# A two-layer decoder step on one core: the dilated attention's last part, the samples' attention and the first output weights in one weave

## The chip, the core and the metric

The kernel runs on one core of a Trainium2 chip. The metric is the device time of one execution in microseconds; the kernel before took 1539.32 us in the median of three runs (1535.01 to 1544.55). The engines are named as in the profile: PE (TensorE, matmuls; PEld its weight loads), DVE (VectorE), ACT (ScalarE), POOL (GpSimd), SP (SyncE, which here only issues DMAs). Each takes its instructions in the order in which they stand in its queue.

## What is computed

Two layers run over 1024 prompt tokens and 32 sample tokens (8 sequences of 4). The first layer is attention. Its path A looks 128 tokens back; its path B has three groups with dilations 1, 4 and 16, whose outputs are merged by their softmax denominators. Cut to what matters here:

```python
def _layer0_out(x, oa, obs, lses, z, w_out, ln_g, ln_b):
    wts = softmax(stack(lses, 0), 0)                    # the three groups of B
    ob = einsum('rbshg,rbshgd->bshgd', wts, stack(obs, 0))
    mix = concatenate([oa.reshape(..), ob.reshape(..)], -1)
    mix = mix * silu(z)                                 # gate path
    y = einsum('bse,ed->bsd', mix, w_out)               # output projection
    return layer_norm(DN_ALPHA * x + y, ln_g, ln_b)
```

The prompt's tokens attend to each other. The samples' tokens attend to caches (128 keys for A and for B's first group, 128 of each dilated one) and to themselves, with the same weights and the same output projection. The second layer (mLSTM) follows.

## The kernel before, in words

All matmuls on activations split each operand into a rounded high part and a rest, and add three products: high by high, high by low, low by high. The tokens lie in three chunks (`CH`): 384, 384 and 288, the last with the 32 samples.

Layer 0 first projects keys and values, then queries (`proj_q`). Path A and the row maxima of B's groups 1 and 2 are woven with the query projections. A second weave (`W2`) joins the gate path (`proj_z0`, 8 feature blocks) with `attention_b`: the maxima of group 3, B's scores for kv=0, and `EARLY` = 9 query blocks of kv=1 (`self.late`). A third weave (`W3`) joins the rest of kv=1, the samples' attention (`sample_attn`) and six merges. Then `out0` loads and splits the eight output weights (`load_wo`) and runs the output projection (`out_proj`, L862) over nine token tiles.

`weave` only fixes the order in which the program's parts are recorded, by shares of work; `ahead` gives a part a priority. A scheduler then makes the order on each engine from priorities, dependencies and its own durations, so the engine order is not that of the code.

For B, `scores` (L462) takes one query block at a time. It loads a mask row for it (`mask_load`, L442: 2 KB into the last partition of `EM`, two buffers in turn, twice 1x4x128). For each of one or two key blocks it runs three matmuls into `sc` (L475, mask L457 or L460, L477), two exponentials on ACT (`ph`, `p`, L481 and L482), the low part `pl` on DVE or, every fourth time, on POOL (L116, L484), and three matmuls into `av` (L488 to L490). `emit` then adds `av` into the result `OD` on DVE (L580, L582). There are 35 such score blocks for each kv, 70 in all. `AB_PS` says which PSUM tags hold `sc` and `av`: four and two buffers in the second weave, two and three in the third. A load of queries (`Q`, 512 KB) serves two query blocks.

The result goes to DRAM chunk by chunk and comes back in `merge0` (L816): `mo` (result), `mf` (denominators, whose reciprocal is taken on DVE, L839, for kv=1), `mz` (gate), a product, then its high part on ACT (`mh`) and its low part on DVE (`ml`). Merges are named by (path, kv, chunk); those of path 1 (B), kv=1, come from `last` when a chunk is finished.

The samples' attention loads the cached keys and values for four sequences at a time into `KT` tiles (`sample_keys`, L660, pool `smt`, 4 buffers). Scores go into `sS` (L682) and through DVE masks; transposes (`pT`, L709 and L710) and values (`so`, L724 and L729) follow, and a transpose back (`oT`, L742).

All DMAs of this part are issued from SP, in the order of its queue; a DMA whose wait is not over holds back those behind it.

Of the kernel before, what the change touches and what calls it, by code (L numbers as in the profile page):

```python
# [4 lines left out]
F32 = mybir.dt.float32  # L5
# [59 lines left out]
W1, W2, W3, W4 = (129, 76), (86, 80), (28, 15, 6), (64, 90)  # L65

EARLY = 9
# [5 lines left out]
ENG = dict(q="scalar", z="scalar")  # L73
# [24 lines left out]
class Builder:  # L98
# [409 lines left out]
    def finish(self, ty, kv, sink_nm=None):  # L508

        nc = self.nc  # L510
        dn = self.sm.tile([32, 128], F32, tag="dn", name="dn")
# [56 lines left out]
    def attn_b(self, kv, done=None):  # L568
# [3 lines left out]
        for g in (3, 2, 1):  # L572
            (K1, K2), V = self.k_load(g, kv), self.v_load(g, kv)

            def emit(qb, av, g=g):
# [7 lines left out]
                if g == 1 and qb in (2, 5, 7):  # L583
                    t = slice(CH[qb // 3][0], 128 * qb + 128)
                    self.store('o', self.OD[1][kv][:, :, t], OD[:, :, t])
                    if done:
                        done(qb // 3)
# [72 lines left out]
    def sample_keys(self, src, g, a, st):  # L660

        out = []
        if g < 2:
            t = st.tile([128, 4, 128], F32, tag="KT", name="KT")
            self.load(t, src[:, 4 * a:4 * a + 4])
            return [t[:, j:j + 1] for j in range(4)]
        for u in range(2):
            t = st.tile([128, 2, 4, 128], F32, tag="KT", name="KT")
# [5 lines left out]
    def sample_group(self, g, st):  # L674

        nc, A = self.nc, self.A
        for a in range(2):
            ks = self.sample_keys(A['kt'][g], g, a, st)
# [24 lines left out]
    def sample_av(self, g, o, sp, st, first, last):  # L703
# [18 lines left out]
        for a in range(2):  # L722
            vs = self.sample_keys(A['vc'][g], g, a, st)
# [26 lines left out]
    def sample_attn(self, sp, st):  # L750
        nc = self.nc
        self.sample_queries(sp)
# [3 lines left out]
        for ty, gs in ((0, (0,)), (1, (1, 2, 3))):  # L756
            for g in gs:
                yield from self.sample_group(g, st)
# [21 lines left out]
            for i, g in enumerate(gs):  # L780
                yield from self.sample_av(g, o, sp, st, i == 0, g == gs[-1])
# [104 lines left out]
    def layer0(self):  # L886
# [24 lines left out]
        with tc.tile_pool(name="qp", bufs=2) as self.qp, tc.tile_pool(name="kp", bufs=2) as self.kp, \  # L911
                tc.tile_pool(name="vp", bufs=2) as self.vp, tc.tile_pool(name="ppool", bufs=3) as self.ppool, \
                tc.tile_pool(name="odp", bufs=1) as self.odp:
            sm = self.sm = tc.alloc_tile_pool(name="sm", bufs=1)
# [11 lines left out]
            self.KZ = [sm.tile([128, TP], F32R, name=f"KZ{u}") for u in range(2)]  # L926
# [4 lines left out]
            self.maskm = sm.tile([128, 4, 128], F32R, name="maskm")  # L931
            self.hi(self.maskm, raw[:, 0:512].rearrange("p (u k) -> p u k", u=4))
            self.EM = [sm.tile([128, 2, 4, 128], F32R, name=f"EM{u}") for u in range(2)]
# [34 lines left out]
            def attention_b():  # L968
# [3 lines left out]
                self.bps = AB_PS[1]  # L972
                yield from self.attn_b(0)
                late = self.late = self.attn_b(1, last)
                for _ in range(EARLY):
                    yield next(late)

            weave((gate_path(), W2[0]), (ahead(tc, attention_b(), AHEAD[1]), W2[1]))
# [3 lines left out]
            self.x2p = tc.alloc_tile_pool(name="x2p", bufs=1, side="right")  # L982
            self.mp = tc.alloc_tile_pool(name="mp", bufs=1, side="right")
            sm.release()
            M = self.M = [(self.xp.tile([128, 8, n], F32R, tag=f"xh{c}", name=f"mh{c}"),
                           self.xp.tile([128, 8, n], F32R, tag=f"xl{c}", name=f"ml{c}"))
                          for c, (t0, n) in enumerate(CH)]

            def merges(cs):
                for c in cs:  # L990
                    for ty, kv in ((0, 0), (0, 1), (1, 0)):
                        self.merge0(ty, kv, c, M)
                        yield 1.0

            self.bps = AB_PS[2]
            with tc.tile_pool(name="smt", bufs=4) as st:
                sp = Scratch(*(self.x2p.tile([128, 3072], F32, tag=f"x{u}x2", name=f"scr{u}") for u in "hl"))
                weave((ahead(tc, self.late, AHEAD[2]), W3[0]), (ahead(tc, self.sample_attn(sp, st), AHEAD[2]), W3[1]),
                      (merges((0, 1)), W3[2]))
            self.merge0(1, 1, 2, M, False)  # L1000
            run(merges((2,)))

    def out0(self):
# [3 lines left out]
        self.wsp = tc.alloc_tile_pool(name="wsp1", bufs=2, side="right")  # L1007
        with tc.tile_pool(name="wo", bufs=1) as wp:
            W = [self.load_wo(A['wo0'], k, *self.wo_tiles(wp, k)) for k in range(8)]
# [629 lines left out]
```

## Time and profile before

| what | before |
|---|---|
| time, median of 3 runs (range) | 1539.32 us (1535.01 to 1544.55) |
| profiled execution, its own time | 1543.16 us |
| its span | 1541.4 us |
| mean granted TensorE clock | 0.961 |
| PE busy | 1431.8 us (93%) |
| DVE busy | 894.1 us (58%) |
| ACT busy | 482.0 us (31%) |
| DMA | 227.33 MB, 147 GB/s in the mean |

The profile shows one execution. Busy times of PE are modelled and overlap in a pipeline, so a matmul's duration is longer than the step to the next one. A granted clock of 1.0 is the upper level (2.4 GHz), 0.5 the lower (1.2 GHz).

### The profile page before, as it was taken

The page shows a single profiled execution, that of the slowest core. Times are in us where ns is not written, and L with a number is a line of the kernel's source. Part 1 is how long each engine was busy: PE and PEld are TensorE (multiplying, and loading weights), DVE is VectorE, ACT ScalarE, POOL GpSimd, SP SyncE. Part 2 cuts the span into 40 slices and gives each one's busy share as a digit, 9 for nine tenths or more (in the row PEclk, how much of TensorE's full clock was granted, in tenths as well). Part 3 has the DMA queues.
Part 4 walks back from the last instruction along what each step waited for, and adds up shares of the span by engine and source line. Part 5 has one row for each costly group of instructions (what it writes and reads, how often), then busy time and mean ns, then how long its engine had stood idle before and what let it go on. Part 6 is the DMA issues. An engine that isn't in the chain of part 4 may idle for free.

```text
span 1541.4 us, 22195 instructions
## 1 busy us (share of the span) xinstructions
PE 1431.8 (93%) x7908; PEld 1216.0 (79%) x7908; DVE 894.1 (58%) x2483; ACT 482.0 (31%) x907; POOL 173.9 (11%) x213
## 2 busy tenths in 40 slices
PE   8998999999897889568999999999999999999997
PEld 8988998889897555136879878888898899877785
DVE  4312455558676777635776436555565565556686
ACT  5332134342122656212104313332233133323310
POOL 1003131212220222000000000000000000000010
PEclk9999999999999989658999999999999999999999
DMA  8444555547753565765311375374214322341741
GB/s 293 166 152 157 191 179 163 166 140 219 198 169 94 174 193 162 220 203 192 124 52 57 118 254 190 117 232 140 77 46 150 109 60 63 109 135 22 233 129 53
DMA packets 140220, 227.33 MB, mean 147 GB/s; under 512 B 17616, under 2 KB 108080, under 8 KB 139592
## 3 DMA queue, kind: packets, MB, share of 16 engines
q1 hardware_dynamic: 132046, 204.55, 43.0%
q10 hardware_dynamic: 8064, 21.37, 3.8%
q8 instruction: 63, 1.03, 0.3%
q14 instruction: 47, 0.39, 0.1%
HBM read 167.06 MB, written 81.88 MB: 162 GB/s over the span
## 4 chain that ended last, share of the span: by engine, by line
PE 70%; DMA 15%; DVE 7%; issue 4%; ACT 2%; POOL 1%; SPq 1%; DVEq 0%; ACTq 0%; POOLq 0%
PE pj L199 10%; PE pj L200 10%; PE pj L201 10%; PE py L165 4%; PE py L166 4%; PE py L167 3%; PE pvo L165 3%; PE pvo L166 3%; PE pvo L167 3%; DMA G<-GR 2%; DMA QZ<-QQ 2%; DMA wr<-in_wo_dram 1%; PE av L488 1%; PE sc L475 1%; PE av L489 1%
## 5 line engine op out<-in xcount | busy, mean ns | idle before, releaser
L199 PE MATMUL pj<-xh,wh 128*128 128x384 f32 (+1 forms) x576 | 188.9, 328 | 9.8 <-DVE sl L117 5.5
L199 PE MATMUL pj<-x1h,wh 128*128 128x384 f32 (+1 forms) x576 | 189.9, 330 | 1.7 <-ACT QT L1166 1.6
L201 PE MATMUL pj<-x1h,wl 128*128 128x384 f32 (+1 forms) x576 | 188.1, 327 | 0.0
L200 PE MATMUL pj<-xl,wh 128*128 128x384 f32 (+1 forms) x576 | 187.9, 326 | 0.0
L200 PE MATMUL pj<-x1l,wh 128*128 128x384 f32 (+1 forms) x576 | 187.7, 326 | 0.0
L201 PE MATMUL pj<-xh,wl 128*128 128x384 f32 (+1 forms) x576 | 187.6, 326 | 0.0
L199 PEld LDWEIGHTS pj<-xh,wh 128*128 128x128 f32 x576 | 110.2, 191 | 14.7 <-DVE sl L117 6.4
L199 PEld LDWEIGHTS pj<-x1h,wh 128*128 128x128 f32 x576 | 108.9, 189 | 6.5 <-issue 3.3
L201 PEld LDWEIGHTS pj<-x1h,wl 128*128 128x128 f32 x576 | 108.7, 189 | 6.0 <-issue 5.8
L200 PEld LDWEIGHTS pj<-x1l,wh 128*128 128x128 f32 x576 | 108.9, 189 | 4.0 <-issue 3.8
L201 PEld LDWEIGHTS pj<-xh,wl 128*128 128x128 f32 x576 | 110.0, 191 | 1.0
L200 PEld LDWEIGHTS pj<-xl,wh 128*128 128x128 f32 x576 | 110.0, 191 | 0.8
L429 DVE CUSTOM_DVE_ANT_0 junk<-st,maskq 128x256 f32<-128x256 f32 (+1 forms) x256 | 93.2, 364 | 24.6 <-PE st L425 9.7
L165 PE MATMUL pvo<-voh,x1h 128*128 128x512 f32 x256 | 101.1, 398 | 2.3 <-DVE SZ L1182 2.3
L166 PE MATMUL pvo<-voh,x1l 128*128 128x512 f32 x256 | 100.4, 395 | 0.0
L167 PE MATMUL pvo<-vol,x1h 128*128 128x512 f32 x256 | 99.6, 392 | 0.0
L481 ACT ACTIVATE ph<-sc 128x512 fp32r<-128x512 f32 x100 | 60.1, 602 | 76.8 <-PE sc L477 60.5
L808 POOL TENSOR_TENSOR rsw<-rsw,mhalf 128x1 f32<-128x1 f32 (+1 forms) x54 | 40.5, 750 | 354.7 <-DVE rsw L807 340.5
L122 POOL TENSOR_TENSOR wl<-wr,wh 128x1024 fp32r<-128x1024 f32 x24 | 58.6, 2443 | 183.2 <-ACT qs L233 136.4
L112 ACT ACTIVATE wh<-wr 128x1024 fp32r<-128x1024 f32 x48 | 50.8, 1058 | 78.3 <-PE pj L200 71.1
L116 DVE TENSOR_TENSOR pl<-p,ph 128x512 fp32r<-128x512 f32 x82 | 59.9, 737 | 20.0 <-ACT p L482 18.1
L425 PE MATMUL st<-K,QZ 128*128 128x256 f32 x256 | 51.7, 289 | 9.7 <-DMA QZ<-QQ 4.9
(352 smaller groups left out, 3129.8 us busy)
## 6 DMA issues: line engine op xcount, KB each, us to landing
Q<-QQ SPq DMA_DIRECT2D x32, 512.0 KB
out_kvs_dram<-in_cache_b_kv_dram SPq DMA_DIRECT2D x16, 1022.0 KB
wr<-in_w0f_dram SPq DMA_DIRECT2D x24, 512.0 KB
wr<-in_w1f_dram SPq DMA_DIRECT2D x24, 512.0 KB
QQ<-sh ACTq DMA_DIRECT2D x16, 512.0 KB
QQ<-sl ACTq DMA_DIRECT2D x16, 512.0 KB
QZ<-QQ SPq DMA_DIRECT2D x32, 256.0 KB
wr<-in_wo_dram SPq DMA_DIRECT2D x16, 512.0 KB
```

What stands on the lines that cost most here:

```text
L112: return self.nc.scalar.activation(out, in_, AF.Copy, scale=scale)
L116: return self.nc.vector.tensor_tensor(out, in_, f(hi), OP.subtract)
L122: self.nc.gpsimd.tensor_tensor(out, in_, f(hi), OP.subtract)
L165: nc.tensor.matmul(ps, xh[:, k, t], wh, start=k == 0, stop=False)
L166: nc.tensor.matmul(ps, xl[:, k, t], wh, start=False, stop=False)
L167: nc.tensor.matmul(ps, xh[:, k, t], wl, start=False, stop=k == 7)
L199: nc.tensor.matmul(ps[:, :n], wh[:, k, :], xh[:, k, :n], start=k == 0, stop=False)
L200: nc.tensor.matmul(ps[:, :n], wh[:, k, :], xl[:, k, :n], start=False, stop=False)
L201: nc.tensor.matmul(ps[:, :n], wl[:, k, :], xh[:, k, :n], start=False, stop=k == 7)
L425: nc.tensor.matmul(st[:, u, :], Q1[:, h, q0:q0 + 128], K1[:, w0:w0 + 256], start=True, stop=True)
L429: nc.vector.tensor_tensor_reduce(junk[:, :n], st[:, u, c0:c0 + n], mk, 1.0, -3e38, OP.add, OP.max, ST[:, 8 * h + qb:8 * h + qb + 1])
L481: nc.scalar.activation(ph, sc, AF.Exp)
```

## The change

`KZ`, `EM` and `maskm` (the key tiles for low parts, the mask rows with their one-hot matrices, and the mask matrices) move from the pool `sm` into a pool `mk` that is released only after B. So `sm` can go before B, which makes room for the merge pool, and for `wsp1`, the pool of weight tiles, which was allocated in `out0`. The second weave now holds only the gate path and the maxima of group 3. The third weave holds all of B (both kv), the samples' attention, the first two output weights and the six merges of chunks 0 and 1. All of B runs with two `sc` buffers and three `av` buffers. The samples' `KT` tiles take the weight tiles of `wsp1` (tags `wh` and `wl` in turn, two buffers each). The first two output weights sit in the same pool. The denominators for kv=0 use a `wraw` tile. The stores of B's result move from SP's queue to ACT's.

```diff
-W1, W2, W3, W4 = (129, 76), (86, 80), (28, 15, 6), (64, 90)
-EARLY = 9
+W1, W2, W3, W4 = (129, 76), (86, 8), (77, 20, 8), (64, 90)
...
-ENG = dict(q="scalar", z="scalar")
+ENG = dict(q="scalar", z="scalar", b="scalar")
...
-        dn = self.sm.tile([32, 128], F32, tag="dn", name="dn")
+        dn = (self.wraw if ty else self.sm).tile([32, 128], F32, tag="wraw" if ty else "dn", name="dn")
...
-                    self.store('o', self.OD[1][kv][:, :, t], OD[:, :, t])
+                    self.store('b', self.OD[1][kv][:, :, t], OD[:, :, t])
...
-    def sample_keys(self, src, g, a, st):
+    def sample_keys(self, src, g, a):
+        def tile(shape):
+            self.nkt += 1
+            return self.wsp.tile(shape, F32, tag="wh" if self.nkt % 2 else "wl", name="KT")
...
+            mk = tc.alloc_tile_pool(name="mk", bufs=1)
...
-            self.KZ = [sm.tile([128, TP], F32R, name=f"KZ{u}") for u in range(2)]
+            self.KZ = [mk.tile([128, TP], F32R, name=f"KZ{u}") for u in range(2)]
...
-            self.maskm = sm.tile([128, 4, 128], F32R, name="maskm")
+            self.maskm = mk.tile([128, 4, 128], F32R, name="maskm")
...
-            self.EM = [sm.tile([128, 2, 4, 128], F32R, name=f"EM{u}") for u in range(2)]
+            self.EM = [mk.tile([128, 2, 4, 128], F32R, name=f"EM{u}") for u in range(2)]
...
-            def attention_b():
+            def maxima_b():
                 for kv in range(2):
                     yield from self.attn_b_stats(3, kv)
                     self.attn_b_max(kv)
-                self.bps = AB_PS[1]
-                yield from self.attn_b(0)
-                late = self.late = self.attn_b(1, last)
-                for _ in range(EARLY):
-                    yield next(late)
-
-            weave((gate_path(), W2[0]), (ahead(tc, attention_b(), AHEAD[1]), W2[1]))
+
+            weave((gate_path(), W2[0]), (ahead(tc, maxima_b(), AHEAD[1]), W2[1]))
             tmp.release()
             stage.release()
             self.wsp.release()
             self.x2p = tc.alloc_tile_pool(name="x2p", bufs=1, side="right")
+            self.wsp = tc.alloc_tile_pool(name="wsp1", bufs=2, side="right")
+            sm.release()
             self.mp = tc.alloc_tile_pool(name="mp", bufs=1, side="right")
-            sm.release()
...
+            self.halves = 0
+
+            def attention_b():
+                for kv in range(2):
+                    yield from self.attn_b(kv, last if kv else None)
+                    self.halves += 1
 
             def merges(cs):
-                for c in cs:
-                    for ty, kv in ((0, 0), (0, 1), (1, 0)):
+                for ty, kv in ((0, 0), (0, 1), (1, 0)):
+                    while self.halves < ty:
+                        yield None
+                    for c in cs:
                         self.merge0(ty, kv, c, M)
                         yield 1.0
 
+            def samples():
+                sp = Scratch(*(self.x2p.tile([128, 3072], F32, tag=f"x{u}x2", name=f"scr{u}") for u in "hl"))
+                yield from self.sample_attn(sp)
+                for k in range(2):
+                    w = [self.wsp.tile([128, 1024], F32R, tag=f"w{u}", name=f"o{u}") for u in "hl"]
+                    self.W0.append(self.load_wo(A['wo0'], k, *w))
+                    yield 0.5
+
+            self.W0 = []
             self.bps = AB_PS[2]
-            with tc.tile_pool(name="smt", bufs=4) as st:
-                sp = Scratch(*(self.x2p.tile([128, 3072], F32, tag=f"x{u}x2", name=f"scr{u}") for u in "hl"))
-                weave((ahead(tc, self.late, AHEAD[2]), W3[0]), (ahead(tc, self.sample_attn(sp, st), AHEAD[2]), W3[1]),
-                      (merges((0, 1)), W3[2]))
+            weave((ahead(tc, attention_b(), AHEAD[1]), W3[0]), (ahead(tc, samples(), AHEAD[2]), W3[1]),
+                  (ahead(tc, merges((0, 1)), AHEAD[1]), W3[2]))
             self.merge0(1, 1, 2, M, False)
             run(merges((2,)))
+            mk.release()
...
-            W = [self.load_wo(A['wo0'], k, *self.wo_tiles(wp, k)) for k in range(8)]
+            W = self.W0 + [self.load_wo(A['wo0'], k, *self.wo_tiles(wp, k)) for k in range(2, 8)]
```

What the scheduler makes of it is seen at three places. Line numbers of the changed kernel differ by a few. On PE, at the end of B, the order before is this (the `sS`, `pT` and `so` rows are the samples'):

```order
L477 MATMUL sc<-Q_6351,KZ_955 128x512
L488 MATMUL av<-ph,V 66x512
L489 MATMUL av<-ph,V 64x512
L682 MATMUL sS<-KT,scrh 32x128 x8
L490 MATMUL av<-pl,V 66x512 x2
L488 MATMUL av<-ph,V 66x512
L489 MATMUL av<-ph,V 64x512
L490 MATMUL av<-pl,V 66x512
L709 MATMUL pT<-ident,scrl 128x128
L710 MATMUL pT<-ident,scrl 32x128
```

All but the first eight matmuls of the samples on cached keys stand behind B's last value matmul. On PE, at the start of kv=1 (group 3), the order of the changed kernel is this:

```order
L475 MATMUL sc<-Q_5609,KZ_957 128x512
L684 MATMUL sS<-KT,scrl 32x512 x2
L488 MATMUL av<-pl,V 66x512
L486 MATMUL av<-ph,V 66x512
L487 MATMUL av<-ph,V 64x512
L684 MATMUL sS<-KT,scrl 32x512 x2
L473 MATMUL sc<-Q_5700,K_5690 128x512
L684 MATMUL sS<-KT,scrl 32x512 x2
L455 MATMUL sc<-EM_965,maskm 128x4x64 x2
L475 MATMUL sc<-Q_5700,KZ_958 128x512
```

The samples' scores stand in ones and twos between B's, and so do their transposes and values further on. On SP, at the same place, the order of the changed kernel is this (`KT` 128x1024 is 512 KB, `Q` the queries, `EM` a mask row):

```order
L104 DMA Q_5700<-QQ_78 128x4x256
L104 DMA KT<-in_kt_dram 128x1024 x2
L104 DMA EM_965<-QQ_78 1x4x128
L104 DMA KT<-in_kt_dram 128x1024
L104 DMA EM_965<-QQ_78 1x4x128
L104 DMA KT<-in_kt_dram 128x1024
L104 DMA EM_966<-QQ_78 1x4x128 x2
L104 DMA Q_5766<-QQ_78 128x4x256
L104 DMA KT<-in_kt_dram 128x1024 x3
L104 DMA EM_965<-QQ_78 1x4x128 x2
```

Before, these loads stood behind B's last mask row on SP; now seven of the eight large key loads are in this piece. On PE, at the end of B, the order of the changed kernel is this (`py` is the output projection; eleven more rows of it stand ahead of the first):

```order
L165 MATMUL py<-ol,mh_4914 128x512
L488 MATMUL av<-pl,V 66x512
L163 MATMUL py<-oh,mh_4914 128x512
L164 MATMUL py<-oh,ml_4915 128x512
L165 MATMUL py<-ol,mh_4914 128x512
L163 MATMUL py<-oh,mh_4914 128x512
L164 MATMUL py<-oh,ml_4915 128x512
L165 MATMUL py<-ol,mh_4914 128x512
L488 MATMUL av<-pl,V 66x512
L486 MATMUL av<-ph,V 66x512
L487 MATMUL av<-ph,V 64x512
L488 MATMUL av<-pl,V 66x512
```

The projection with weights 0 and 1 (24 matmuls over tiles 0 and 1 and two column halves) begins ahead of B's last five value matmuls; before, it began behind the samples' last transpose `oT`.

## Rows read from the trace of the kernel before

**Rows 1.** The page: the span, and two rows of the 40 slices.
```profile
span 1541.4 us, 22195 instructions
...
PE   8998999999897889568999999999999999999997
...
PEclk9999999999999989658999999999999999999999
```

**Rows 2.** Busy time by stage: window, length, engines, granted clock, DMA share, GB/s.
```profile
core 0: us, PE busy (x) PEld busy (x) DVE busy (x) ACT busy (x) POOL busy (x), PEclk, DMA share, GB/s
...
500.00:565.00 65.00, 55.44 (x212) 34.76 (x212) 47.19 (x69) 40.72 (x75) 16.17 (x14) 0.92 0.66 190
565.00:621.00 56.00, 49.98 (x202) 32.51 (x201) 37.73 (x58) 35.26 (x65) 11.34 (x9) 0.92 0.57 160
621.00:632.00 11.00, 3.52 (x21) 1.29 (x21) 10.02 (x12) 0.55 (x2) 1.26 (x1) 0.69 0.60 183
632.00:694.00 62.00, 35.32 (x245) 15.48 (x246) 29.79 (x62) 11.92 (x34) 3.06 (x2) 0.56 0.70 219
694.00:725.00 31.00, 25.71 (x97) 20.17 (x97) 13.27 (x18) 8.67 (x10) 0.52 (x1) 0.84 0.60 200
```

**Rows 3.** The same view in windows of 10 us.
```profile
580.00:590.00 10.00, 8.73 (x42) 5.78 (x42) 5.21 (x11) 6.33 (x12) 2.37 (x2) 1.00 0.99 263
...
650.00:660.00 10.00, 5.55 (x14) 0.82 (x16) 3.30 (x9) 0.04 (x1) 1.80 (x1) 0.62 0.94 294
```

**Rows 4.** The chain that ended last: start, length, what.
```profile
499.04 1.75 DMA EM<-QQ
...
547.73 4.98 DMA EM<-QQ
...
632.98 4.27 DMA mf<-OD
...
647.07 8.47 DMA KT<-in_kt_dram
...
677.38 5.54 DMA KT<-in_vc_dram
...
695.63 9.32 DMA wr<-in_wo_dram
```

**Rows 5.** ACT in order of time: start, length, engine, line.
```profile
499.62 0.33 ACTq L109 DMA_DIRECT2D SZ<-sz  x1
...
620.79 0.59 ACT L482 ACTIVATE p<-sc 128x512 f32<-128x512 f32 x1
```

**Rows 6.** PE in order of time.
```profile
605.49 0.39 PE L475 MATMUL sc<-Q,K 128*128 128x512 f32 x1
...
619.41 0.40 PE L475 MATMUL sc<-Q,K 128*128 128x512 f32 x1
...
723.70 1.07 PE L167 MATMUL py<-ol,mh 128*128 128x512 f32 x4
```

**Rows 7.** DVE in order of time.
```profile
632.71 0.96 DVE L117 SCALAR_TENSOR_TENSOR ml<-mz,mh 128x768 fp32r<-128x768 f32 x1
...
637.27 4.96 DVE L839 RECIPROCAL mf<-mf 128x384 f32<-128x384 f32 x2 [3.46 <-DMA mf<-OD]
...
663.20 1.75 DVE L839 RECIPROCAL mf<-mf 128x256 f32<-128x256 f32 x1 [0.36 <-DMA mf<-OD]
...
694.38 1.22 DVE L116 TENSOR_TENSOR ol<-wr,oh 128x1024 fp32r<-128x1024 f32 x1
```

**Rows 8.** SP's issues in order of time.
```profile
546.34 0.43 SPq L106 DMA_DIRECT2D mz<-SZ  x1
547.08 0.56 SPq L106 DMA_DIRECT2D mo<-OD  x1
```

**Rows 9.** DMA issues from 480 to 720 us: count, KB each.
```profile
KT<-in_kt_dram SPq DMA_DIRECT2D x8, 512.0 KB
...
KT<-in_kt_dram SPq DMA_DIRECT2D x4, 256.0 KB
```

More of the change, by code (lines that the diff above doesn't have):

```diff
@@ L658, in sample_queries @@
             self.smx.append(sp.tile([128, 2], F32, tag=f"sm{g}", name="smx"))
-    def sample_keys(self, src, g, a, st):
+    def sample_keys(self, src, g, a):
+        def tile(shape):
+            self.nkt += 1
+            return self.wsp.tile(shape, F32, tag="wh" if self.nkt % 2 else "wl", name="KT")
         out = []
         if g < 2:
-            t = st.tile([128, 4, 128], F32, tag="KT", name="KT")
+            t = tile([128, 4, 128])
             self.load(t, src[:, 4 * a:4 * a + 4])
@@ L667, in sample_keys @@
         for u in range(2):
-            t = st.tile([128, 2, 4, 128], F32, tag="KT", name="KT")
+            t = tile([128, 2, 4, 128])
             s = 4 * a + 2 * u
@@ L672, in sample_keys, with sample_group @@
         return out
-    def sample_group(self, g, st):
+    def sample_group(self, g):
         nc, A = self.nc, self.A
         for a in range(2):
-            ks = self.sample_keys(A['kt'][g], g, a, st)
+            ks = self.sample_keys(A['kt'][g], g, a)
             w = 128 * (1 if g < 2 else 4)
@@ L701, in sample_exp, with sample_av @@
                                  accum_out=den[:, a:a + 1])
-    def sample_av(self, g, o, sp, st, first, last):
+    def sample_av(self, g, o, sp, first, last):
         nc, A = self.nc, self.A
@@ L722, in sample_av @@
         for a in range(2):
-            vs = self.sample_keys(A['vc'][g], g, a, st)
+            vs = self.sample_keys(A['vc'][g], g, a)
             nc.tensor.matmul(o[:, a, :], pN[:, 128 * a:128 * a + 128], self.VS[:, 128 * g:128 * g + 128],
@@ L748, in sample_out, with sample_attn @@
                 nc.vector.tensor_copy(dst.rearrange("p c (s t) -> p c s t", t=4), src)
-    def sample_attn(self, sp, st):
+    def sample_attn(self, sp):
         nc = self.nc
+        self.nkt = 0
         self.sample_queries(sp)
@@ L757, in sample_attn @@
             for g in gs:
-                yield from self.sample_group(g, st)
+                yield from self.sample_group(g)
             m = self.smx[gs[0]]
@@ L780, in sample_attn @@
             for i, g in enumerate(gs):
-                yield from self.sample_av(g, o, sp, st, i == 0, g == gs[-1])
+                yield from self.sample_av(g, o, sp, i == 0, g == gs[-1])
             self.sample_out(o, rec, ty, sp)
@@ L1006, in out0 @@
         self.mp.release()
-        self.wsp = tc.alloc_tile_pool(name="wsp1", bufs=2, side="right")
         with tc.tile_pool(name="wo", bufs=1) as wp:
-            W = [self.load_wo(A['wo0'], k, *self.wo_tiles(wp, k)) for k in range(8)]
+            W = self.W0 + [self.load_wo(A['wo0'], k, *self.wo_tiles(wp, k)) for k in range(2, 8)]
             with tc.tile_pool(name="lnc", bufs=1) as lc:
```

## The prediction

> **What bounds the kernel now.** I read the page's 40 slices first [rows 1]. TensorE's granted clock is at 9 tenths nearly everywhere and falls to 8, 9, 6, 5, 8 in the slices from about 540 to 730 us. Everything before and after is a PE-bound run of matmuls that this change leaves as it is, so the question is what the hole around 640 us is worth. The table by stage [rows 2] cuts it: 500 to 621 us is B's attention (65 of its 70 score blocks), 632 to 694 the samples' attention and the merges, 694 to 725 the first two tiles of the output projection. From 632 to 694 PE is busy for 35.3 of 62 us, at a clock of 0.56: mostly the lower level, 1.2 of 2.4 GHz. The chain [rows 4] shows why: it goes through loads of the samples' keys and values (8.47 and 5.54 us), the denominators (4.27 us) and the first output weights (9.32 us), each followed by little work. Nothing there fills TensorE. DMA is the busiest resource, 0.70 of its share.
>
> I measure from the end of the last exponential of B, 621.4 us [rows 5], to the end of the first two output tiles, 723.70 + 1.07 = 724.8 us [rows 6]: **103.4 us**. The two tiles themselves are 96 matmuls; at the spacing of B's matmuls (next paragraph, 0.23 us) they need 22 us. About 81 us are tail.
>
> Inside B, the score blocks' first matmuls go from 605.49 to 619.41 us in 10 steps [rows 6]: 1.39 us for a block of six matmuls, 0.23 us each, with two score buffers, the setting that all of B gets now. 65 blocks at that pace are 90 us, and 121 were spent: **31 us of slack** lie in B, scattered.
>
> **The change, part by part.**
>
> *The tail that goes.* All matmuls of the samples (the rows on KT, pT, sNew, oT) now stand between B's scores and values on PE, as the order shows; behind the last value matmul comes the output projection at once, with its weights 0 and 1 ready (24 of the 96 matmuls, 5.5 us, some of them ahead of B's last value matmuls, where PE waits anyway). What then sets the end of tiles 0 and 1 is VectorE, since the low halves of weights 2 to 7 queue behind the late merges. The last merge chain before: the denominators of chunk 1 land at 632.98 + 4.27 = 637.3 us [rows 4], their two reciprocals take 4.96 us [rows 7], so they are done at 642.2, 21 us behind the last exponential. I take that chain as unchanged, since B's last additions and the store that it waits for are unchanged too. Behind it VectorE's order has, up to the low half of weight 7: six low halves at 1.22 us = 7.3, three operations on a chunk of 768 columns at 0.96 = 2.9, two reciprocals at 1.75 = 3.5 [rows 7], and half a dozen shorter ones on chunk 2 that I put at 3 us by their size. 21 + 17 = 38 us. The four remaining weight loads (9.32 us from issue to landing for the first one before, [rows 4]) run beside this and can add a few us; four closing matmuls add 1. I take **42 us** instead of 103.4: 61 us less. Bounds: 33 us if the merges no longer wait (11 us of last values plus 22 of matmuls), 58 if the weight loads wait behind them (two rounds of 9.3 us behind 38).
>
> *Work moved into B: PE.* The samples' matmuls are 35.3 us of busy PE at 0.56 of the clock [rows 2], so about 20 us at full clock. Against 31 us of slack, they cost between 0 (all fall into gaps) and 20 (none does).
>
> *Work moved into B: DMA.* Keys and values of the samples are 8 loads of 512 KB and 4 of 256 KB [rows 9], and as many for the values: 10.5 MB, plus 1 MB for the two output weights. At 650 to 660 us the engines moved 294 GB/s at a share of 0.94 [rows 3], 313 GB/s at full share, so 11.5 MB are 37 us of all engines. B holds 0.66 x 65 + 0.57 x 56 = 75 us of DMA already [rows 2]: 112 of 121, which would just fit. It is uneven. In the second half (565 to 621, kv=1) come the 16 large loads and the output weights, 9.4 MB or 30 us, beside 0.57 x 56 = 32: 62 us in 56. At a share of 0.95 that half takes 65, **9 us longer**. That a full DMA need not stop PE is seen at 580 to 590 us [rows 3]: share 0.99, PE still 8.73 of 10. Upper end, nothing hidden: 37 us.
>
> The two costs overlap in part; of B's stretching I take **18 us**: the 9 of DMA and half of the 20 of PE less 1 for gaps that the new work keeps at the upper clock. Range 3 to 45.
>
> *Small parts.* The stores of B's result go from SP's queue to ACT's. An issue there took 0.33 us [rows 5]; six, with a wait each for VectorE's addition, are 2 to 5 us on ACT, which is busy 41 of 65 and 35 of 56 us in B [rows 2]: nothing, and up to 5 us in the range if exponentials queue behind such a wait. VectorE's work for the samples is less than the 29.8 us that it is busy from 632 to 694, merges included, and B leaves it 36 of 121 us idle: hidden. Weights 0 and 1 now sit in the buffers of the next layer's first weights until the last output tile, so those are split later: one ACT and one VectorE operation of 1.2 us behind about 21 remaining matmuls (4.8 us): 0 to 2, I take **1**. The pools themselves cost nothing; fewer score buffers (2 instead of 4 for the first half) are priced by the 1.39 us, which had two.
>
> **Sum.** 1543.2 us (profiled execution; its span is 1541.4) - 61 + 18 + 1 = 1501. The median of the runs shown, 1539.3, is 3.9 below that execution, so I expect **1497** as the median of new runs.
>
> **A rule against the change.** A mask row of 2 KB landed 1.75 us after its issue at 499 us, and 4.98 us at 547.73, right behind two loads for a merge [rows 4, 8]; B needs a fresh row for each query block and has two buffers for it. The Trainium skill, "DMA: Bandwidth & Descriptors", section "Queues, rings and completion order", says that on each DMA engine the descriptors of one issuing queue are consumed in ring order; by it every large load on SP's queue delays the mask rows and queries behind it in full, and the trace's two durations agree in direction.
>
> **Rivals.**
> 1. *Forecast*: the tail goes, B stretches by 10 to 28 us: 1487 to 1507. **0.50**.
> 2. *B becomes bound by its queue*: the 16 large loads stand ahead of mask rows and queries on SP, each for 524 KB / 313 GB/s = 1.7 us, none hidden: 27 us, plus the 9 of PE: B is 36 longer, 1515; with a tail nearer its upper bound up to 1523. For it: the 4.98 us row. Against: 580 to 590 us. **0.24**.
> 3. *All hidden*: B stretches by less than 10, 1478 to 1487. For it: 31 us of slack, and a clock of only 0.92 in B that denser work could lift. Against: the 9 us of DMA. **0.12**.
> 4. *Gain and loss near each other*: the tail at 58 us and B stretched by 36 or more, 1524 to 1555. **0.08**.
> 5. *Slower*: the samples' matmuls stand in PE's one queue ahead of B's scores, so a late key tile stops all of B. Before, PE waited in that place for nobody; a pair of 512 KB loads took 8.47 us [rows 4]. Eight pairs waited for in full are 68 us, with 20 of PE 88 in place of 18: 1567. It decides from a mean wait of 5 us a pair (8 x 5 + 20 + 1 = 61), and from 7 us it is over 1% slower. **0.06**. Against: the loads are issued several blocks ahead of their matmuls in SP's order.
>
> That the change does not do what it says (the samples left behind B) is excluded by the order. One per cent, 15 us, is about what a measurement of this kernel can tell from no change. Faster by more than that (below 1524): cases 1 to 3, with 0.86 less a little of case 2's upper edge: **0.83**. Within: **0.10**. Slower: **0.07**. For 8 in 10 I leave out about a half of case 3's lower edge and cases 4 and 5: **1480 to 1523**.
>
> **What the new profile would show.** Right: no slice with a clock of 5 or 6 around 640 us; samples' matmuls of about half their former duration; tiles 0 and 1 done about 40 us behind the last exponential, with PE waiting for the low halves of weights; DMA share of 0.8 or more in B's second half. Wrong: waits of scores for mask rows or queries, or of the samples' matmuls for KT, that sum to over 40 us; or a gap of over 20 us between B's last value matmul and weight 2.

## The result and the profile after

| | before | changed |
|---|---|---|
| median of 4 runs (range) | 1537.72 us (1535.01 to 1544.55) | 1522.13 us (1519.43 to 1522.62) |
| ratio to before, 95% interval | | 0.9888 (0.9853 to 0.9924) |
| again, 4 runs beside other runs of before | 1538.60 us | 1517.77 us, 0.9861 (0.9840 to 0.9882) |
| again, 5 runs | 1538.50 us | 1519.37 us, 0.9876 (0.9854 to 0.9897) |

The change gains 16 to 21 us. The forecast was 42 (1497): right in sign, and the time lies inside the range, but over half of the gain was missing. The page of the changed kernel: its span and two rows of the 40 slices, to be held beside [rows 1].

```profile
span 1520.8 us, 22193 instructions
...
PE   8998999999898898958999999999999999998997
...
PEclk9999999999999897979999999999999999999999
```

The hole at 6 and 5 tenths of the clock is gone, and PE's thin slice is now one (the 5, from 646 to 684 us). The clock still falls to 7 tenths in two slices, from 570 to 608 us and from 646 to 684 us. Busy time by stage (window, length, then PE, PEld, DVE, ACT, POOL, the granted clock, DMA share, GB/s), to be held beside [rows 2]:

```profile
500.00:565.00 65.00, 59.51 (x289) 34.84 (x287) 47.21 (x84) 38.07 (x74) 11.75 (x11) 0.97 0.79 229
565.00:621.00 56.00, 47.35 (x227) 25.70 (x224) 34.24 (x61) 24.57 (x53) 10.46 (x8) 0.79 0.82 227
621.00:650.00 29.00, 28.17 (x167) 18.30 (x168) 15.52 (x24) 19.55 (x36) 5.63 (x5) 1.00 0.56 173
650.00:662.00 12.00, 6.22 (x17) 3.50 (x16) 10.03 (x10) 0.84 (x1) 0.31 (x1) 0.72 0.12 33
662.00:702.00 40.00, 23.46 (x78) 17.81 (x78) 24.43 (x25) 9.53 (x11) 1.26 (x1) 0.83 0.75 217
```

From 650 to 662 us there is almost no transfer (share 0.12), and from 662 to 702 a heavy one: the tail waits for something before it loads. ACT in order of time gives the end of B's exponentials, 648.30 + 0.59 = 648.9 us, to be held beside [rows 5]:

```profile
648.30 0.59 ACT L480 ACTIVATE p<-sc 128x512 f32<-128x512 f32 x1
...
667.89 2.00 ACT L110 ACTIVATE oh<-wr 128x1024 fp32r<-128x1024 f32 x2 [7.60 <-DMA mz<-SZ]
682.06 1.06 ACT L110 ACTIVATE oh<-wr 128x1024 fp32r<-128x1024 f32 x1 [5.91 <-DMA wr<-in_wo_dram]
```

**Account.** The last exponential of B ends 27.5 us later (648.9 against 621.4, [rows 5]); forecast +18. From there to the first matmul of the third output tile, at 702.24 us, are 53.3 us, and from the same point to the end of tiles 0 and 1 were 103.4 before [rows 5, 6] (the third tile followed at once there): 50 less; forecast 61 less. Behind it 2 us are lost. 50 - 27.5 - 2 = 20.5; the spans differ by 20.6. In the two repeats the last exponential ends at 645.3 and 646.2 us (+23.9 and +24.8) and the tail (from the end of the last exponential to the third tile) is 51.5 and 52.6 us.

The forecast's 42 us went to the end of tiles 0 and 1. That end, 695.72 + 1.07 = 696.8 us, lies 47.9 us behind the last exponential. The remaining 5.45 us are a wait of the third tile for VectorE, for which the forecast had no term. PE in order of time:

```profile
695.72 1.07 PE L165 MATMUL py<-ol,mh 128*128 128x512 f32 x4
702.24 0.80 PE L163 MATMUL py<-oh,mh 128*128 128x512 f32 x1 [5.45 <-DVE xr L883]
```

### The profile page after: what moved, and what is told of

It reads as the page before. It is cut to its first block, busy times and chain, and to the rows that moved or that the text cites. A ratio compares the mean times of both kernels' runs of the same rounds, so it can differ in the third digit from the quotient of the medians.

```text
span 1520.8 us, 22193 instructions
## 1 busy us (share of the span) xinstructions
PE 1425.6 (94%) x7908; PEld 1208.7 (79%) x7908; DVE 895.5 (59%) x2483; ACT 482.9 (32%) x907; POOL 173.0 (11%) x213
## 4 chain that ended last, share of the span: by engine, by line
PE 67%; DMA 18%; DVE 8%; issue 3%; ACT 2%; SPq 1%; POOL 1%; DVEq 0%; ACTq 0%; POOLq 0%
PE pj L197 10%; PE pj L198 10%; PE pj L199 10%; PE py L163 3%; PE py L165 3%; PE py L164 3%; PE pvo L163 3%; DMA G<-GR 3%; PE pvo L164 3%; PE pvo L165 3%; DMA EM<-QQ 2%; DMA QZ<-QQ 1%; DMA KT<-in_kt_dram 1%; DMA out_cmems_dram<-Cs 1%; PE st L423 1%
## 5 line engine op out<-in xcount | busy, mean ns | idle before, releaser
L197 PEld LDWEIGHTS pj<-xh,wh 128*128 128x128 f32 x576 | 108.7, 189 | 17.4 <-DVE sl L115 7.7
L163 PE MATMUL py<-oh,mh 128*128 128x512 f32 x128 | 54.8, 428 | 20.1 <-ACT oh L110 11.3
```

The costliest lines, as they stand in the source:

```text
L163: nc.tensor.matmul(ps, xh[:, k, t], wh, start=k == 0, stop=False)
L197: nc.tensor.matmul(ps[:, :n], wh[:, k, :], xh[:, k, :n], start=k == 0, stop=False)
```

## The experiments

All kernels are the changed one with one edit, except where a run says otherwise (samples_loads_on_pool has two). For B I read one row of busy time each, from the start of its first to the start of its last high exponential. From it: idle is length less PE's busy time, work at full clock is busy time by the granted clock (a mean over the window, so good to about 3 us), and the rest of the busy time is lost to the lower clock. Each row is of one execution; over the three of the changed kernel, length varies by 5.6 us, idle time and work by less than 1. The row (window, length, PE busy, clock, DMA share, GB/s) of before:

```profile
486.90:620.30 133.40, 113.37 (x454) 0.92 0.59 171
```

The same of the changed kernel:

```profile
481.50:647.80 166.30, 145.45 (x717) 0.90 0.75 220
```

The same of its first repeat, and then of the second:

```profile
482.70:644.20 161.50, 141.32 (x717) 0.93 0.76 227
```
```profile
484.40:645.10 160.70, 139.91 (x718) 0.94 0.76 228
```

| kernel | B's length | idle | work at full clock | lost to the clock | median, ratio (interval) |
|---|---|---|---|---|---|
| before | 133.4 | 20.0 | 104.3 | 9.1 | |
| changed | 166.3 | 20.9 | 130.9 | 14.5 | 1522.13, 0.9888 |
| repeat 1 | 161.5 | 20.2 | 131.4 | 9.9 | 1517.77, 0.9861 |
| repeat 2 | 160.7 | 20.8 | 131.5 | 8.4 | 1519.37, 0.9876 |
| no_samples | 139.8 | 28.5 | 101.3 | 10.0 | 1490.68, 0.9692 (0.9663 to 0.9720) |
| one_kt_load | 153.9 | 17.4 | 124.3 | 12.3 | 1510.94, 0.9824 (0.9792 to 0.9855) |
| thin_mm | 161.0 | 24.6 | 125.5 | 10.9 | 1506.06, 0.9797 (0.9760 to 0.9833) |
| spread | 176.0 | 30.5 | 128.1 | 17.5 | 1531.57, 0.9952 (0.9931 to 0.9972) |
| mask_row_on_pool | 182.0 | 31.0 | 132.9 | 18.1 | 1536.52, 0.9982 (0.9960 to 1.0004) |
| row_and_query_on_pool | 192.1 | 39.5 | 134.3 | 18.3 | 1553.83, 1.0087 (1.0059 to 1.0115) |
| samples_loads_on_pool | 168.9 | 25.1 | 130.8 | 12.9 | 1515.03, 0.9851 (0.9827 to 0.9875) |
| even_extra_work | 146.0 | 22.9 | 113.3 | 9.9 | 1500.81, 0.9749 (0.9728 to 0.9769) |

**What makes B longer: the work, the loads, or the rest?** Theory P: TensorE's own work. Theory D: the loads and their queue.

```diff
 def samples():  # no_samples
-    yield from self.sample_attn(sp)
+    self.OS = sp.tile([128, 8, 32], F32, name="OSs")
+    nc.gpsimd.memset(self.OS, 1.0)
```


> The samples' attention is left out of the weave (their rows of the merge get ones), all else stays; so the outputs of the sample rows are not the reference's. Every theory: B's last exponential returns from 648.9 to 621-624 us, since the before kernel's B without them ended at 621.4, and the total falls by about 27 us to 1494-1498. If B still ends later than 630, the loss comes from the merges or the first two output weights, which also moved into B, and not from the samples.


```diff
 def sample_keys(self, src, g, a):  # one_kt_load, g >= 2
-    for u in range(2): t = tile([128, 2, 4, 128]); self.load(t, src[:, s:s + 2]); ...
+    if not hasattr(self, 'kt1'):
+        self.kt1 = tile([128, 2, 4, 128]); self.load(self.kt1, src[:, 0:2])
+    return [self.kt1[:, 0], self.kt1[:, 1]] * 2
```


> All of the samples' matmuls stay, but the 16 loads of 512 KB for the two dilated groups become one (the tile is used 16 times), so 7.9 MB leave B's queue; the sample rows are not the reference's. Theory P (TensorE's work of about 20 us at full clock lands as it is, because it stands in 12 blocks and not in the gaps): B ends 0 to 4 us earlier. Theory D (the loads fill the DMA engines and the mask rows and queries queue behind them, and the waits then take the clock down): B ends 12 to 22 us earlier, and no slice between 554 and 608 us shows a granted clock below 0.9.


```diff
 # thin_mm
-            w = 128 * (1 if g < 2 else 4)
+            w = 128
-            for r in range(n):
+            for r in range(1):
```


> All 16 loads of 512 KB stay, but the dilated groups' score matmuls take 128 of 512 columns and the value matmuls one of four residues, which takes about 5 + 4 us of TensorE's busy time away (7.5 us for 32 of the one, about 6 us for 80 of the other); the sample rows are not the reference's. Theory P: B ends 8 to 12 us earlier, more where the clock was at half. Theory D: B ends 0 to 3 us earlier, and the half clock stays in two stretches of 10 to 15 us.

Without the samples the total falls by 27 to 31 us, to 1490.7 (below the 1494 to 1498 expected), and B ends 21 to 25 us earlier. But B's length is still 139.8, 6 us over before, with 28.5 us idle in place of 20.0. The two halves of B (kv=0, then kv=1) of before, and below them those of no_samples, show where:

```profile
486.90:554.80 67.90, 55.77 (x224) 0.94 0.60 179
554.80:620.30 65.50, 57.60 (x231) 0.91 0.58 164
```
```profile
483.50:550.50 67.00, 54.76 (x220) 0.92 0.63 183
550.50:623.30 72.80, 56.52 (x220) 0.91 0.60 169
```

The first half, where the score buffers went from four to two, is no longer than before and idles as much (12.2 and 12.1 us). The second idles 16.3 us in place of 7.9. One wait there, in PE's order of time, is that long: the first score of a group waits 9.26 us for its 512 KB of queries, issued behind keys, values and the merges' denominators.

```profile
578.59 1.19 PE L473 MATMUL sc<-Q,K 128*128 128x512 f32 x2 [9.26 <-DMA Q<-QQ]
```

In the three executions of the changed kernel TensorE's waits for queries in B sum to 2.0 us at most, so with the samples this hole is gone.

With 7.9 MB fewer to load, B is 7 to 12 us shorter (D said 12 to 22, P 0 to 4). With thin_mm's fewer columns its last exponential ends at 645.9 us, 3.0 us earlier than in the first execution of the changed kernel and level with the repeats (P said 8 to 12, D 0 to 3), though about 7 of the samples' 30 us of matmul work are gone (its row holds nearly 2 us of output projection). That its total is 12 to 16 us lower comes in the main from the tail, which is 45.7 us there (6 to 8 us less, see below), and from 3 to 4 us behind it. Neither theory holds alone. The table gives the shares: before to changed, work at full clock grew by 27 us and idle time by less than 1, in all three executions. The loss to the clock explains 5 us of the first execution only (below, the last section).

I had put the samples' work at 20 us, not 27. A part of the difference is how it is cut. PE in order of time, the dilated groups' scores (four sequences in four column tiles) in the changed kernel, and then in one_kt_load, which waits for no tile between them:

```profile
558.36 1.05 PE L684 MATMUL sS<-KT,scrl 128*32 128x512 f32 x4
559.34 0.50 PE L455 MATMUL sc<-EM,maskm 128*128 128x256 f32 x2
...
565.88 1.14 PE L684 MATMUL sS<-KT,scrl 128*32 128x512 f32 x8
566.95 0.39 PE L455 MATMUL sc<-EM,maskm 128*128 128x256 f32 x1
```
```profile
564.35 1.92 PE L682 MATMUL sS<-KT,scrl 128*32 128x512 f32 x16
566.21 0.39 PE L455 MATMUL sc<-EM,maskm 128*128 128x256 f32 x1
```

Four matmuls occupy PE for 0.98 us, eight for 1.07, sixteen for 1.86. The changed kernel has the 32 in seven pieces, 7.0 us; one_kt_load in two, 3.7. That is 3.3 of the 7 us by which its work is smaller than the changed kernel's; the other half I can't place.

**Does placing the samples earlier help?**

```diff
-AHEAD = (1000, 1000, 60, 300)
+AHEAD = (1000, 1000, 1000, 300)
```


> Same work, but the samples' instructions get the same lead in the order as B's own (1000 in place of 60), so that their first matmuls stand at block 8 instead of 22, the dilated groups' loads at the mask rows of blocks 12 to 35, and their last matmul at block 40 instead of 60. Theory P: the work takes as long wherever it stands, B ends within 4 us of 648.9. Theory D: the loads have a longer stretch for the same bytes, B ends 6 to 15 us earlier and the total is 1508 to 1516. If their matmuls now wait for loads at the head of TensorE's queue, B ends later.

B is 10 to 15 us longer. The loads had more room, and the waits went elsewhere: for queries 7.6 us, and 8.8 us for VectorE's copies into `OD` (6.5 of them in one wait; another copy had itself waited 5.9 us for a DMA). Both theories miss: D forecast a gain, P no change. The third case, scores of the samples that wait for their key tiles, is not it either: those waits are 0.3 us.

**Is it the queue?**

```diff
 def mask_load(self, g, kv, qb):  # mask_row_on_pool
-            self.load(f(E[127:128, u]), r.unsqueeze(0))
+            (self.nc.gpsimd if g else self.nc.sync).dma_start(f(E[127:128, u]), r.unsqueeze(0))
```


> The mask rows of B (2 KB each, two for a block of queries) are issued by POOL on a queue of its own instead of SP's, where they stand behind the samples' 512 KB loads; the 512 KB query loads stay on SP. The planner then also puts the samples' matmuls earlier (blocks 8 to 38). Theory D in its ring form (a small load waits for the bytes ahead of it in its own queue): the scores' waits for mask rows (10.0 us between 482 and 662 in the changed kernel) fall under 2 us, and B ends 6 to 12 us earlier. In its bandwidth form (all queues share 16 busy engines): the waits stay over 6 us and B ends within 4 us of 648.9.


```diff
 def q1_load(self, g, kv, hf, tag="Q1"):  # row_and_query_on_pool: the edit above, and
-        self.load(f(Q1), ...)
+        (self.nc.gpsimd if g else self.nc.sync).dma_start(f(Q1), ...)
```


> As the run before, and the queries of B (512 KB, four for a group and key head) go with the mask rows on POOL's queue, so that SP's holds the samples' loads, the merges' and the keys and values. Ring form of D: B ends 10 to 16 us earlier (both waits go). Bandwidth form: under 4 us earlier, the waits being for queries and rows as before. POOL's own low halves (every fourth block) stand behind its issues: if an issue takes over 2 us there, waits of the value matmuls for POOL show over 10 us and B is longer than 166 us.


```diff
 def sample_keys(self, src, g, a):  # samples_loads_on_pool, both loads
-            self.load(t, src[...])
+            self.nc.gpsimd.dma_start(t, src[...])
-POOL_LO = 4
+POOL_LO = 1000
```


> The other way round: the samples' key and value loads (20 loads, 9.4 MB) are issued by POOL, which may stand waiting for a free tile, and POOL's share of the low halves goes to VectorE; mask rows and queries keep SP. Ring form of D: B ends 8 to 16 us earlier. Bandwidth form: within 4 us. VectorE's 16 more subtractions are 0.66 us each, 11 us of an engine that is not full: under 3 us.

PE's waits between 482 and 662 us in the changed kernel (line, releaser: total, times, longest), then in mask_row_on_pool up to 668 us, and in row_and_query_on_pool up to 670 us:

```profile
PE sc L458 <- DMA EM<-QQ: 5.3, 5, 2.8
PE sc L455 <- DMA EM<-QQ: 4.7, 4, 1.7
...
PE av L486 <- ACT ph L479: 2.7, 4, 0.8
```
```profile
PE sc L473 <- DMA Q<-QQ: 13.1, 4, 5.3
...
PE sc L458 <- DMA EM<-QQ: 1.1, 2, 0.8
```
```profile
PE av L486 <- ACT ph L479: 14.4, 14, 4.7
PE av L488 <- DVE pl L114: 10.8, 10, 4.6
...
PE sc L455 <- DMA EM<-QQ: 1.6, 3, 0.9
```

The same waits of before, between 486 and 621 us:

```profile
PE sc L475 <- DMA Q<-QQ: 6.3, 5, 2.0
PE sc L457 <- DMA EM<-QQ: 6.3, 7, 1.8
```

A mask row on its own queue is hardly late: 10.0 us of waits become 1.1 (mask_row_on_pool), and with the queries moved too 1.8 for both. This agrees with small loads that wait behind the large ones of their queue. It does not show it alone, because the order changed too: in all three runs the scheduler (the planner of the expectations) put the samples earlier. Their long scores begin at 531.8, 529.5 and 538.8 us, in the changed kernel at 554.9. Nor are such waits new: before, without the samples' loads in B, they summed to 12.6 us.

B gets longer, 182 and 192 us. With the rows alone moved, the queries left on SP are late, 13.1 us in place of none; with both moved, waits for exponentials and low halves take the place. The reverse, the samples' loads on POOL (and POOL's low halves on VectorE), leaves 14 us of waits for rows and queries (6.0 + 4.9 + 3.1) and B at 168.9, where 8 to 16 us less were forecast by the ring form. The Trainium skill, "DMA: Bandwidth & Descriptors", section "Issuing engines are not separate DMA queues", says that DMAs of all issuers run on the same 16 engines and that a second issuer saves only issue time. The last run agrees: its B is no shorter than the 160.7 to 166.3 us of the changed kernel. Its total, 1515, is not told apart from the repeats (intervals overlap). What remains open is a mask row on another queue with the samples left in place.

**Can B's idle time take work at all?**

```diff
 # even_extra_work, on top of no_samples
-                nc.tensor.matmul(av[0:64], V[:, kb, 0:64], ph, ...)
+                for _ in range(2 if g else 1):
+                    nc.tensor.matmul(av[0:64], V[:, kb, 0:64], ph, ...)
```


> B without the samples (as in the run no_samples), but each of its 70 blocks does its second value matmul twice (0.21 us each at full clock, 15 us together; the low halves of V count double in B, so its outputs are not the reference's). So the extra work is spread evenly, one piece to a block, and waits for nothing. If the samples' work lengthened B because it stands in bunches, away from TensorE's idle time (28.5 us in no_samples), evenly spread work goes into it: B grows by 0 to 6 us from 139.8. If the idle time lies where any extra matmul of TensorE's order only pushes the rest (its waits are for exponentials and additions that themselves start later), B grows by 11 to 16 us.

12.0 us of work, one piece to a block, made B 6.2 us longer and took 5.6 us out of its idle time: between the two answers. About half is absorbed when it is evenly spread and waits for nothing. (The median is 10 us over that of no_samples, so 4 us of it lie outside B and are not explained.) The samples, beside the same no_samples, brought 30 us of work and took about 8 us of idle time, a quarter, which is about the length of the one wait for queries that is gone with them.

**What holds the tail at 53 us?** VectorE in order of time in the changed kernel: reciprocals, the last addition into `OD`, the low half of weight 2, and further on VectorE's additions for tiles 0 and 1 (`xr`).

```profile
650.26 2.55 DVE L842 RECIPROCAL mf<-mf 128x384 f32<-128x384 f32 x1 [4.79 <-DMA mf<-OD]
653.28 2.54 DVE L842 RECIPROCAL mf<-mf 128x384 f32<-128x384 f32 x1
...
661.08 0.69 DVE L580 TENSOR_TENSOR OD<-av,OD 65x512 f32<-65x512 f32 x1 [1.67 <-PE av L488]
666.10 4.96 DVE L842 RECIPROCAL mf<-mf 128x384 f32<-128x384 f32 x2 [3.47 <-DMA mf<-OD]
670.98 1.16 DVE L114 TENSOR_TENSOR ol<-wr,oh 128x1024 fp32r<-128x1024 f32 x1
...
699.31 1.00 DVE L846 TENSOR_TENSOR mz<-mz,scrh 128x64 f32<-128x64 f32 x1 [1.15 <-DMA mz<-SZ]
...
701.51 2.47 DVE L883 SCALAR_TENSOR_TENSOR xr<-xr,py 128x512 f32<-128x512 f32 x4
```

And pieces of the chain that ended last:

```profile
661.08 0.69 DVE OD L580
661.80 5.78 DMA OD<-OD
667.60 0.36 SPq L104
...
669.90 7.22 DMA xr<-in_xtok_dram
```

Chunk 0's denominators make VectorE wait 4.79 us and divide 5.1 us while the last low halves and additions of B stand behind. So the last addition comes at 661.08, 12 us after the last exponential, and its store lands at 667.6. At that moment SP issues the layer norm's loads (667.60) and ACT splits weights 2 and 3 (667.89): in the code their tiles are allocated after B's `OD` is released. (Here the profile names a gate load as what ends ACT's wait; in the four kernels with the later store, below, it names the store of `OD`.) PE's two long waits for weights follow:

```profile
669.00 0.80 PE L163 MATMUL py<-oh,mh 128*128 128x512 f32 x1 [5.52 <-ACT oh L110]
...
683.17 0.79 PE L163 MATMUL py<-oh,mh 128*128 128x512 f32 x1 [5.81 <-ACT oh L110]
```

The third tile then waits for `xr`, which stands on VectorE behind the merges of chunk 2, whose last gate load (`mz`) lands at 699.2 us. The early division itself is not new. In the kernel before VectorE had it in the same place, and the last addition came at 631.73 us, 10.3 us behind the last exponential:

```profile
621.98 4.96 DVE L839 RECIPROCAL mf<-mf 128x384 f32<-128x384 f32 x2 [4.02 <-DMA mf<-OD]
...
631.73 0.68 DVE L582 TENSOR_TENSOR OD<-av,OD 65x512 f32<-65x512 f32 x1
```

```diff
 def load_wo(self, src, k, h, l):  # tail_low_on_pool, weights 2 to 7
-        self.lo(l, raw, h)
+        self.nc.gpsimd.tensor_tensor(l, raw, f(h), OP.subtract)
```


> Only the tail: the low halves of output weights 2 to 7 are made by POOL, idle there, instead of VectorE, whose reciprocals and merge stand ahead of them, so that the two raw weight buffers come free earlier. If the 11 us by which the tail missed the forecast (53.3 instead of 42) hang on this chain, the time from the last exponential to the matmul after tiles 0 and 1 falls to 42-47 us and the total by 6 to 11 us. If the weights were only waiting behind the merge's loads and the last stores on SP's queue, it falls by 0 to 3 us.


```diff
 # store_two_pieces, in attn_b; store_one_piece has {7: (0, 1, 2)}
-                if g == 1 and qb in (2, 5, 7):
-                    t = slice(CH[qb // 3][0], 128 * qb + 128)
+                at = {5: (0, 1), 7: (2,)} if kv else {2: (0,), 5: (1,), 7: (2,)}
+                if g == 1 and qb in at:
+                    t = slice(CH[at[qb][0]][0], 128 * qb + 128)
                     self.store('b', self.OD[1][kv][:, :, t], OD[:, :, t])
```


> Key head 1's output of B is stored in two pieces (the first two chunks of tokens together behind block row 5, the third at the end) instead of three, so that chunk 0's denominators can't be asked for before, and the planner puts both reciprocals behind the last low halves and the last additions into OD on VectorE. Theory T (VectorE waits 4.79 us for chunk 0's denominators and divides 5 us, with the last additions behind it until 661.1; then the last store, and the memory under OD, which the layer norm's and the weights' tiles take, comes free at 667.6): last addition at about 652, last store landed at 656 to 659, first of the layer norm's loads there instead of 667.6, and tile 2 begins 44 to 48 us after B's end instead of 53.3; total 6 to 10 us less. Rival (the tail is the sum of DMA bytes and VectorE's 21 us of division in any order): 0 to 2 us less.

> The same with one store of all three chunks at the end: the last addition at about 652 too, but 1.06 MB then go in one store and land at 660 to 662, and every division waits for it. Theory T: tile 2 begins 48 to 52 us after B's end, total 2 to 6 us less than the changed kernel. Rival: no less, or 2 to 5 us more, because nothing of the merge runs ahead of the store.

> The store in two pieces together with the samples' loads on POOL's queue. If the two gains have separate causes they add: 12 to 16 us less than the changed kernel, 1506 to 1511. If the 7 us of the loads on POOL came from the tail as well (3 us of them did), 8 to 11 us less.

> The store in two pieces together with the output weights' low halves 2 to 7 on POOL. The latter alone gave 0.9 us of the tail, since the weights themselves came late. If with an earlier store the low halves behind VectorE's divisions are what TensorE waits for (5.49 and 4.50 us in the run with two pieces), tile 2 begins 38 to 42 us after the last exponential's start instead of 46.0 and the total is 1504 to 1510. If the loads' bytes are next (5.6 MB from the store on), it begins after 44 to 46 and the total is 1511 to 1514.

| kernel | last exponential ends | third tile begins | tail | median, ratio (interval) |
|---|---|---|---|---|
| changed, and its repeats | 648.9, 645.3, 646.2 | 702.24, 696.83, 698.74 | 53.3, 51.5, 52.6 | above |
| tail_low_on_pool | 647.2 | 699.61 | 52.4 | 1523.52, 0.9904 (0.9877 to 0.9931) |
| store_two_pieces | 643.3 | 688.21 | 44.9 | 1513.49, 0.9834 (0.9804 to 0.9863) |
| store_one_piece | 653.0 | 697.74 | 44.8 | 1513.31, 0.9839 (0.9810 to 0.9868) |
| two_pieces_and_pool_loads | 652.3 | 696.61 | 44.3 | 1512.64, 0.9834 (0.9801 to 0.9866) |
| two_pieces_low_on_pool | 652.3 | 697.33 | 45.1 | 1514.47, 0.9832 (0.9808 to 0.9856) |

The low halves on POOL change nothing. The later store takes 6 to 9 us off the tail in all four kernels that have it, in one piece too, where I expected less. VectorE, ACT and SP of store_two_pieces:

```profile
647.31 0.69 DVE L580 TENSOR_TENSOR OD<-av,OD 65x512 f32<-65x512 f32 x1 [4.36 <-PE av L488]
655.43 4.96 DVE L844 RECIPROCAL mf<-mf 128x384 f32<-128x384 f32 x2 [7.43 <-DMA mf<-OD]
```
```profile
648.03 0.85 ACTq L107 DMA_DIRECT2D OD<-OD  x1
652.04 2.00 ACT L110 ACTIVATE oh<-wr 128x1024 fp32r<-128x1024 f32 x2 [8.78 <-DMA OD<-OD]
```
```profile
652.01 0.82 SPq L104 DMA_DIRECT2D lng<-in_ln_dram  x2
```

The reciprocals now stand behind the last addition, that is 4.0 us behind the last exponential (643.3) instead of 12, and the layer norm's loads and the split of the weights begin with the landing of the last store: 8.7 us behind it instead of 18.7. In all sixteen profiled executions of the changed kernel and its variants the third tile begins 37.5 to 41.2 us behind the start of the last addition, so the tail is shorter by about as much as this addition comes earlier behind the last exponential (in thin_mm, too, where it comes 8 us behind). The landing alone does not set it: in store_one_piece ACT's split begins only 12.8 us and the layer norm's loads 15.8 us behind the last exponential, and the tail is as short. Within those 40 us the loads and VectorE's order act together. In store_two_pieces PE waits 5.49 and 4.50 us for low halves; with those on POOL it waits 3.42 and 7.42 us for high halves instead, and the tail stays (45.1). Of the 6 to 9 us about 4 show in the median: 1 to 5 us come back behind the third tile's begin (818.6 to 819.1 us to the end in the changed kernel's three executions, 819.8 to 823.6 in these four). The gains of two_pieces_and_pool_loads don't add (5 us less than the repeat beside it, where 8 to 16 were expected), since the loads on POOL gain nothing that can be told from zero.

**The repeats** stand in the tables above. The first is 2 us below what I expected, the second inside.


> The changed kernel itself, beside the three runs that follow on the same chip: 1520 to 1526 us.

> The changed kernel beside it, on the same chip: 1517 to 1523 us.

The best kernels found are the four with the later store, which can't be told apart: 1512.64 to 1513.49 us beside 1517.77, and 1514.47 beside 1519.37. That is 4 to 5 us less than the changed kernel beside them, where the intervals still touch.

## Why the prediction was right and wrong

*Right: the tail goes.* The samples' stage vanished behind B, no slice near 640 us shows a clock of 5 or 6, and the samples' long score matmuls take 605 ns, 1060 before, about half as forecast by the clock. The change is faster, by 1.1 to 1.4%.

*Wrong, the step of the tail: "21 us behind the last exponential. I take that chain as unchanged".* The start of that chain did stay (chunk 1's reciprocals end at 671.06 us, 22 us behind the last exponential). What failed is that "the four remaining weight loads (...) run beside this and can add a few us". They could not: the splits of weights 2 and 3 and the layer norm's loads began only when the last store of `OD` landed, 18.7 us behind the last exponential, and the two raw buffers are refilled only when VectorE has made the low halves behind its divisions (loads issued at 672.17). PE waits for high halves, not for low halves as I forecast: 5.52 us for the split that began with that landing, and 5.81 us for the next weight's load. So tiles 0 and 1 ended 47.9 us behind the last exponential, not 42. A wait that the sum left out came on top: 5.2 to 5.5 us of the third tile for VectorE's `xr`. The term was 61 and measured 50 to 52 with it. Undoing the order on VectorE gave 6 to 9 of the missing 9 to 11.

*Wrong, the step of B: "the 9 of DMA and half of the 20 of PE".* 18 us was the sum; 24 to 27.5 were measured. TensorE's work grew by 27 us, not 20, and the idle time did not shrink. The 9 us for DMA did not show as waits: PE's waits for DMA in B sum to 11 us, against 12.6 before, and 7.9 MB fewer took 3 us off the idle time. The half that I let vanish in gaps is what evenly spread work loses there (even_extra_work); but what else moved into B, the merges and the first weights with their loads, opened 8.5 us of new idle time first (no_samples, in one wait for queries), and the samples took about as much back. So the saving was spent before it was made. Which of those loads made the queries late no run separates. Scaling a stage's busy time by the clock was too low as well; 3 us of it go with the cut into short pieces, the rest stays open.

*Rival 2* gave 1515 to 1523, where the time now lies, but by another way: it had B bound by mask rows behind the loads. These waits are 10.0 us, not 27, and no more than before (12.6), and taking them away, with the samples then earlier, did not help. So the range held the time for a reason other than the one that had put its upper part there: the two main terms were off by 6 to 11 us each, in the same direction. The rule that I weighed there fits in direction (the row on another queue is hardly late) and did not decide the time. *Rival 5*, matmuls that wait for key tiles, is at 1.1 us. The loads' share is 0.82 from 565 to 621 us, as forecast.

*Back of the sum:* +1 forecast behind the tail, 2 measured.

## What to carry to other kernels

Work moved into a busy stage costs what it weighs on the engine that bounds the stage, unless a measured gap is shown to take it. Price the gaps after the move, because the other parts that move in make gaps and fill them too. When a tail is shortened, ask which memory its first loads need and who frees it last; here an early division, harmless in the kernel before, stood ahead of B's last additions on VectorE and so ahead of the next stage's loads.

## What the runs showed of the hardware

Matmuls of 32 output columns in four column tiles: four of 128x512 hold PE for 0.98 us, eight for 1.07, sixteen for 1.86. So a piece that is half as long is not half the price. A stretch at the lower clock can cost more than the wait ahead of it. In the first execution of the changed kernel PE waited 2.83 us for a mask row up to 600.41 us, and the clock was 0.51 from 600 to 610 us; that is 9.59 x 0.49 = 4.7 us of busy time lost. In the two repeats the wait of the same matmul was 0.27 and 0.53 us, and the clock was 1.00. The row (window, length, PE busy, clock, DMA share, GB/s) of the first execution, and that of the first repeat:

```profile
600.00:610.00 10.00, 9.59 (x34) 0.51 0.57 127
```
```profile
600.00:610.00 10.00, 8.99 (x47) 1.00 0.73 203
```

That the longer wait brought the clock down is what the three executions suggest; no run varied it alone.
